# Norm rows by DMA, a late second norm and another order of issue in a hybrid RG-LRU / Mamba-2 layer

## The chip, the core and the metric

The kernel runs on one core of a Trainium2 chip. The core has a matrix engine (TensorE, PE), a vector engine (VectorE, DVE), a scalar engine (ScalarE, ACT), GpSimd (POOL) and SyncE (SP), each with its own in-order stream of instructions, and 16 DMA engines. Engines wait for each other by semaphores. On-chip data lies in SBUF, 128 partitions wide; matmul results go to PSUM. The metric is the device time of one execution in microseconds (us).

## The reference

One decoder layer on 2048 tokens of width 1024, all in fp32. A shared input projection feeds two groups of heads; their normalised outputs go through one output projection; a gated FFN of width 2816 follows. Each sub-layer has an RMS norm ahead and one behind it:

```python
h = rms_norm(x, pre_mix_norm[li]);  proj = h @ w_in[li]
lx = causal_depthwise_conv(lru_x, ...);  lh = rg_lru(lx, ...)        # gated recurrence over time
y_lru = rms_norm(lh * gelu(lru_gate), lru_out_norm[li])
xbc = silu(causal_depthwise_conv(ssd_xbc, ...))                      # x, B, C of Mamba-2
y = ssd_chunked(sx * dt[..., None], dt * A, sB, sC) + ssd_d * sx     # chunks of 128 tokens
y_ssd = rms_norm(y * silu(ssd_z), ssd_out_norm[li])
x = x + rms_norm(concatenate([y_lru, y_ssd]) @ w_out[li], post_mix_norm[li])
h = rms_norm(x, pre_ffn_norm[li])
x = x + rms_norm((silu(h @ w_gate[li]) * (h @ w_up[li])) @ w_down[li], post_ffn_norm[li])
```

`rms_norm(x, w)` is x times 1/sqrt(mean of x^2 over the width + 1e-6), times w.

## The kernel before

An fp32 product is made of three faster ones: each operand is split into a high and a low part (fp32r), and `mm3` (L136 to L139) adds hi*hi, lo*hi and hi*lo. ACT casts the high part (L132), DVE subtracts for the low one (L133). A product of the input projection is 128 output channels by 1024 tokens, 48 such matmuls of 512 columns.

The program runs in stages. Tokens come in two blocks of 1024. For each block: the Mamba-2 group (time steps dt, then B, C, then eight pairs of heads, each with a projection X and a gate Z), then the RG-LRU group. Then the output projection over 16 tiles of 128 tokens with the norm behind it, the residual and the norm ahead of the FFN; then gate and up products by Strassen's scheme (seven products instead of eight), and the down product in the same scheme. Operands of the FFN go through DRAM (`h_dr`, `f_dr`, `t_dr`).

The norm ahead of the input projection is applied after the product for the first block: the product of the unnormalised x is multiplied by `rsb`, a 128 x 1024 tile in whose every row stand the 1/rms values of the block's 1024 tokens (L295, L308). Its values come from `rms_of` (L115 to L121: eight one-column matmuls L118, then a short chain for the root) as `rtok`, a token per partition and a chunk per column. `spread` (L153 to L159) turns these into rows: DVE multiplies the identity by a column (L155), and a matmul with a matrix of ones (L158) puts the diagonal into all partitions. ACT copies the result to `rsb` (L627). For the second block `normed` (L573) uses `spread` for two half rows and multiplies x itself (L580).

Two PSUM pools serve the first half of the program: `pp` and `pq`, two buffers each. The first three products (dt, B, C) stand in pp, pp and pq; the next, X0, takes the first pp buffer that comes free, and Z0 the second, which is free once B has been multiplied by `rsb`. Weights come through four `raw` tiles (SP's queue), and split into four `s_hi` and four `s_lo` tiles.

The time-step sums (`ssd_dt3`, L436 to L460) go to DRAM as `cs_dr` (L450) and come back for every pair of heads as `L` (L511), one row to all partitions; from it the decay factors are made. In `ssd_mix` the transposes L514, state products L530, reads L542 and outputs L551 stand between the projections.

In the output stage (L785 to L822) a token tile goes through two norms: the first behind the projection (L811 Square, L813), the second ahead of the FFN (L816 Square, L818), and then through transposes into `h_dr`. For the last tile of each half of the second block the normed rows go to `hl_dr` instead (L821) and are taken up in the gate stage by `late_rows` (L855). Meanwhile `build_op` (L709) splits the first block's operands for the gate stage (casts L717, subtractions L718 into `hx` and `hy`).

At the end, `second_half` (L1043) closes each token tile: sum of the last product (L1089), its Square on ACT (L1025), multiply by the norm's gains (L1026), the root, the residual, the output.

What sets the order: the Python code says what depends on what. The framework's scheduler then lays down the stream of each engine, from its own costs of each instruction and the priorities that the code gives. `order` rows below are these streams.

## Time and profile before

| | |
|---|---|
| median of 3 runs | 2635.73 us (2632.55 to 2636.6) |
| profiled execution | 2635.64 us, its span 2633.8 us |
| PE busy | 2613.7 us (99%) |
| DVE busy | 1852.7 us (70%) |
| ACT busy | 1123.6 us (43%) |
| DMA | 357.79 MB, mean 136 GB/s |

The span is the time from the first to the last instruction in the profiled execution; the rest of its time lies around it. Busy times come from the records of single instructions. Matmuls are pipelined: a matmul of 512 columns has a record of some 0.39 us, but one starts every 0.227 us, so that start-to-start times count. Where an engine stands idle, the profile names what it waited for: in a row such as "PE pq L514 <- DVE t L546" the matmul of line 514 into a `pq` tile waited for DVE's operation of line 546 on a `t` tile.

### The profile page before, as it was taken

To read this page: it belongs to the slowest core of one execution; us is meant where nothing else is said; L and a number is where in the kernel's file an instruction comes from. 1 tells how busy PE (TensorE), PEld (TensorE's weight loads), DVE (VectorE), ACT (ScalarE), POOL (GpSimd) and SP (SyncE) were. 2 spreads that over 40 slices of the span, in tenths; PEclk is the share of its full clock that TensorE was granted. 3 is DMA by queue.
4 is the path that set the end of the run, shared out by engine and by line. 5 is a ranking of instruction groups with operands and counts; after the bars stand their busy time and mean duration, and the time that the engine had idled before them with its cause. 6 is when DMAs were issued, how large, how long until landed. Compare 5 with 4: busy or idle time off the path is not lost.

```text
span 2633.8 us, 31866 instructions
## 1 busy us (share of the span) xinstructions
PE 2613.7 (99%) x12360; PEld 2170.4 (82%) x12360; DVE 1852.7 (70%) x2716; ACT 1123.6 (43%) x1340; POOL 1.1 (0%) x8
## 2 busy tenths in 40 slices
PE   9999999999999999999999999999999999999998
PEld 7888888888888887888877888888888888888887
DVE  7997878888777767544478777678767675334676
ACT  6544456754535777332253222234222222322443
POOL 0000000000000000000000000000000000000000
PEclk9999999999999999999999999999999999999999
DMA  5342461223334635543454333235333325444664
GB/s 211 111 131 73 128 201 65 82 88 113 95 96 150 210 96 205 154 136 123 143 196 150 134 104 116 81 121 195 104 100 110 106 92 173 151 139 153 212 245 140
DMA packets 189975, 357.79 MB, mean 136 GB/s; under 512 B 18528, under 2 KB 91616, under 8 KB 189824
## 3 DMA queue, kind: packets, MB, share of 16 engines
q1 hardware_dynamic: 88912, 256.56, 30.3%
q10 hardware_dynamic: 100912, 99.20, 10.8%
q8 instruction: 97, 1.59, 0.2%
q14 instruction: 54, 0.44, 0.1%
HBM read 253.86 MB, written 101.84 MB: 135 GB/s over the span
## 4 chain that ended last, share of the span: by engine, by line
PE 93%; DVE 3%; ACT 2%; DMA 1%; issue 1%; DVEq 0%; ACTq 0%; SPq 0%
PE pf L139 16%; PE pf L138 16%; PE pf L137 16%; PE pp L137 11%; PE pp L139 10%; PE pp L138 10%; PE pq L137 3%; PE pq L138 3%; PE pq L139 3%; PE pq L530 1%; PE pq L542 1%; PE pq L551 1%; DMA t_dr<-L 1%; PE pq L514 1%; DVE t L399 0%
## 5 line engine op out<-in xcount | busy, mean ns | idle before, releaser
L137 PE MATMUL pp<-hx,s_hi 128*128 128x512 f32 x1392 | 548.2, 394 | 1.2 <-ACT hx L243 0.7
L139 PE MATMUL pp<-hx,s_lo 128*128 128x512 f32 x1392 | 545.4, 392 | 0.5 <-DVE s_lo L133 0.5
L138 PE MATMUL pp<-hx,s_hi 128*128 128x512 f32 x1392 | 543.6, 391 | 0.6 <-DVE hx L244 0.6
L132 ACT CAST s_hi<-raw 128x1024 fp32r<-128x1024 f32 (+1 forms) x167 | 170.3, 1022 | 380.2 <-PE pp L138 123.0
L139 PEld LDWEIGHTS pp<-hx,s_lo 128*128 128x128 f32 x1392 | 261.7, 188 | 56.5 <-issue 0.9
L137 PEld LDWEIGHTS pp<-hx,s_hi 128*128 128x128 f32 x1392 | 261.8, 188 | 56.2 <-issue 1.6
L138 PEld LDWEIGHTS pp<-hx,s_hi 128*128 128x128 f32 x1392 | 261.9, 188 | 54.2 <-DVE hx L244 1.0
L139 PE MATMUL pf<-hx,s_lo 128*128 128x512 f32 x704 | 273.9, 389 | 0.7 <-DVE s_lo L133 0.7
L137 PE MATMUL pf<-hx,s_hi 128*128 128x512 f32 x704 | 274.2, 389 | 0.4 <-ACT s_hi L132 0.4
L138 PE MATMUL pf<-hx,s_hi 128*128 128x512 f32 x704 | 273.9, 389 | 0.0
L133 DVE TENSOR_TENSOR s_lo<-raw,s_hi 128x1024 fp32r<-128x1024 f32 (+1 forms) x167 | 198.0, 1187 | 64.1 <-ACT s_hi L132 55.7
L978 DVE TENSOR_TENSOR d_lo<-draw,d_hi 128x1024 fp32r<-128x1024 f32 (+1 forms) x110 | 121.5, 1129 | 171.4 <-ACT d_hi L977 170.1
L132 ACT CAST s_hi<-S 128x1024 fp32r<-128x1024 f32 x86 | 90.3, 1050 | 268.6 <-PE pf L138 247.3
L138 PE MATMUL pf<-d_lo,d_hi 128*128 128x512 f32 x504 | 196.1, 389 | 0.0
L977 ACT CAST d_hi<-draw 128x1024 fp32r<-128x1024 f32 (+1 forms) x110 | 104.9, 980 | 213.5 <-PE pf L138 181.6
L139 PE MATMUL pf<-d_hi,d_lo 128*128 128x512 f32 x504 | 195.9, 389 | 0.0
L137 PE MATMUL pf<-d_hi 128*128 128x512 f32 x504 | 194.6, 389 | 0.0
L139 PEld LDWEIGHTS pf<-hx,s_lo 128*128 128x128 f32 x704 | 132.1, 188 | 28.9 <-DVE s_lo L133 1.6
L137 PEld LDWEIGHTS pf<-hx,s_hi 128*128 128x128 f32 x704 | 132.1, 188 | 28.2 <-ACT s_hi L132 0.9
L138 PEld LDWEIGHTS pf<-hx,s_hi 128*128 128x128 f32 x704 | 132.1, 188 | 27.4
L302 DVE SCALAR_TENSOR_TENSOR lx<-xr,pk,lx 128x1024 f32<-128x1024 f32 x108 | 138.2, 1279 | 10.4 <-ACT lx L299 9.3
L138 PE MATMUL pf<-hy,s_hi 128*128 128x512 f32 x356 | 138.8, 390 | 1.5 <-DVE hy L718 1.4
(339 smaller groups left out, 4518.2 us busy)
## 6 DMA issues: line engine op xcount, KB each, us to landing
raw<-w_gu_dram SPq DMA_DIRECT2D x86, 512.0 KB, 4.2
f_dr<-fo ACTq DMA_DIRECT2D x154, 256.0 KB, 4.5
raw<-w_in_dram SPq DMA_DIRECT2D x72, 512.0 KB, 3.4
draw<-f_dr SPq DMA_DIRECT2D x57, 512.0 KB, 4.3
L<-cs_dr SPq DMA_DIRECT2D x32, 512.0 KB, 5.3
g_dr<-t ACTq DMA_DIRECT2D x32, 512.0 KB, 3.4
raw<-g_dr SPq DMA_DIRECT2D x32, 512.0 KB, 5.0
raw<-h_dr SPq DMA_DIRECT2D x26, 512.0 KB, 4.4
```

What stands on the lines that cost most here:

```text
L132: a.copy(out=hi, in_=raw)
L133: v.tensor_sub(out=lo, in0=raw, in1=hi.bitcast(F32))
L137: te.matmul(o, lhsT=wh, rhs=hi, start=start, stop=False)
L138: te.matmul(o, lhsT=wh, rhs=lo, start=False, stop=False)
L139: te.matmul(o, lhsT=wl, rhs=hi, start=False, stop=stop)
L302: v.scalar_tensor_tensor(out=y, in0=xr[:, k:k + TB], scalar=cw(k), in1=y, op0=ALU.mult, op1=ALU.add)
L514: te.transpose(pt[:, c].rearrange("p j d -> p (j d)"), xc[:, c * P:(c + 1) * P], ident)
L530: te.matmul(pst[:, c, :], lhsT=Bt[:, c, :], rhs=xe[:, c].rearrange("p j d -> p (j d)"), start=True, stop=True)
L542: te.matmul(po[:, c, :], lhsT=(sc[:, xi, :] if c == 0 else U[:, c - 1, :]), rhs=C[:, c * P:(c + 1) * P], start=True, stop=True)
L551: te.matmul(py[64 * j:64 * j + 64, c, :], lhsT=xd[:, c, j, :], rhs=L[:, j, c, :], start=True, stop=True)
L977: a.copy(out=hi, in_=r)
L978: v.tensor_sub(out=lo, in0=r, in1=hi.bitcast(F32))
```

## The change

Five things change:

- `put_norm` and `get_norm` take the place of `spread`: one transpose makes the 8 x 128 row block, DVE copies it, a DMA writes it to DRAM (`r_dr`), and another reads it back to all partitions.
- The time-step sums (`ssd_dt3`) are called after the first X projection instead of ahead of `ssd_group2`, and use a `t4` tile.
- The second norm of the last token tile of each half is made in the gate stage from `x1_dr` (`late_norm`), in gate steps 3 and 5; its transposes follow in steps 4 and 6, with the gains put on by ACT.
- In the tail the last multiply writes into the PSUM tile of the product (`room`) instead of in place.
- The scheduler is told to use its detailed model of the machine (`schedule_with_timeline_sim=True`), so that the order on every engine is laid anew.

```diff
-    def spread(r, lo, n, tmp):
-        dg = tmp.rearrange("p (c t) -> p c t", t=P)[:, 0:n]
-        v.tensor_tensor(out=dg, in0=bc(ident[:, None, :], [P, n, P]), in1=bc(r[:, lo:lo + n, None], [P, n, P]), op=ALU.mult)
-        ps = pq.tile([P, TB], F32, name="pq")
-        for h in range(n // 4):
-            te.matmul(ps[:, h * HB:(h + 1) * HB], lhsT=ones, rhs=tmp[:, h * HB:(h + 1) * HB], start=True, stop=True)
-        return ps
+    def put_norm(b, row_tile):
+        ps = pq.tile([P, NC, P], F32, name="pq")
+        te.transpose(ps[0:NC, 0, :], rtok[:, b, :], ident)
+        row = row_tile()[0:NC, :]
+        v.tensor_copy(out=row, in_=ps[0:NC, 0, :])
+        sy.dma_start(out=r_dr[b], in_=row)
+
+    def get_norm(out, b, lo, n):
+        sy.dma_start(out=out, in_=r_dr[b, lo:lo + n].rearrange("c t -> (c t)").partition_broadcast(P))
...
-            ps = spread(rtok[:, b], 4 * hh, 4, t4())
+            rw = t4()[:, 0:HB]
+            get_norm(rw, b, 4 * hh, 4)
...
-        a.copy(out=rsb, in_=spread(rtok[:, 0], 0, NC, t4()))
+        put_norm(0, lambda: tp.tile([P, P], F32, name="r_row", bufs=1))
+        get_norm(rsb, 0, 0, NC)
...
-                if gi == 0:
-                    dts = ssd_dt3(b, *dtq)
-                    acc = tl.tile([P, TB], F32, name="acc", bufs=1)
                 grp = ssd_group2(*BC)
                 for i in range(4):
                     xs = ssd_proj(b, 4 * gi + i, hT)
+                    if gi + i == 0:
+                        dts = ssd_dt3(b, *dtq)
+                        acc = tl.tile([P, TB], F32, name="acc", bufs=1)
...
+                if b + 1 < NB and i == 2:
+                    put_norm(1, lambda: tp.tile([P, P], F32, name="r_row", bufs=1))
...
-            a.activation(out=junk, in_=mx, func=AF.Square, accum_out=ss[:, 1:2])
-            rstd_of(ss[:, 1:2], rs[:, 1:2], 1)
-            v.scalar_tensor_tensor(out=xnt, in0=mx, scalar=rs[:, 1:2], in1=gpf, op0=ALU.mult, op1=ALU.mult)
             b, i, j = t // NC, t % 4, (t % NC) // 4
-            if b + 1 == NB and i == 3:
-                a.dma_start(out=hl_dr[j], in_=xnt)
-            else:
+            if b + 1 < NB or i < 3:
+                a.activation(out=junk, in_=mx, func=AF.Square, accum_out=ss[:, 1:2])
+                rstd_of(ss[:, 1:2], rs[:, 1:2], 1)
+                v.scalar_tensor_tensor(out=xnt, in0=mx, scalar=rs[:, 1:2], in1=gpf, op0=ALU.mult, op1=ALU.mult)
                 turn.append(lambda b=b, i=i, j=j, xnt=xnt: turned(b, i, j, xnt))
...
+        def late_norm(j, res):
+            r = [res() for _ in range(2)]
+            t0 = (NB - 1) * TB + j * HB + 3 * P
+            ss = small.tile([P, 2], F32, name="o_ss")
+            rs = small.tile([P, 2], F32, name="o_rs")
+            for q in range(2):
+                sy.dma_start(out=r[q], in_=x1_dr[t0:t0 + P, q * HB:(q + 1) * HB])
+                a.activation(out=res(), in_=r[q], func=AF.Square, accum_out=ss[:, q:q + 1])
+            v.tensor_add(out=ss[:, 0:1], in0=ss[:, 0:1], in1=ss[:, 1:2])
+            rstd_of(ss[:, 0:1], rs[:, 0:1], 1)
+            for q in range(2):
+                v.tensor_scalar(out=r[q], in0=r[q], scalar1=rs[:, 0:1], scalar2=None, op0=ALU.mult)
+            return r
...
-                a.copy(out=xs[-1], in_=ps)
+                for k in range(4):
+                    c = slice(k * P, (k + 1) * P)
+                    a.activation(out=xs[-1][:, c], in_=ps[:, c], func=AF.Copy, scale=par("g_ffn", 4 * q + k))
...
-                if b + 1 < NB and 3 <= fi < 5:
-                    late_rows(fi - 3, res)
+                if b + 1 < NB and fi in (3, 5):
+                    late = late_norm((fi - 3) // 2, res)
+                if b + 1 < NB and fi in (4, 6):
+                    late_rows((fi - 4) // 2, late, res)
...
-            v.tensor_mul(out=y[:, t], in0=y[:, t], in1=pfw[:, e * HB:(e + 1) * HB])
+            v.tensor_mul(out=y[:, t] if room is None else room, in0=y[:, t], in1=pfw[:, e * HB:(e + 1) * HB])
...
-            second_half((m1, u2), t, 0, 0, ms[t], xq[t])
+            second_half((m1, u2), t, 0, 0, ms[t], xq[t], p)
...
-    with tile.TileContext(nc) as tc:
+    with tile.TileContext(nc, schedule_with_timeline_sim=True) as tc:
```

Rows of an order below are instructions of one engine in the order of issue: line, operation, output<-inputs with buffer numbers, shape, and xN for N alike. Lines of the changed kernel are its own (L155 there is the transpose in `put_norm`, L424 stands for L422, L516 for L514, L544 for L542, L553 for L551, L724 for L718).

First place: PE in the first projection X0 (`pp_613`, now `pp_590`) and at the head of Z0 (`pp_690`, now `pp_667`). Before:

```order
L138 MATMUL pp_613<-hx_243,s_hi_616 128x512
L158 MATMUL pq_460<-t4_458,ones_118 128x512 x2
L139 MATMUL pp_613<-hx_242,s_lo_617 128x512
...
L138 MATMUL pp_613<-hx_354,s_hi_616 128x512
L139 MATMUL pp_613<-hx_353,s_lo_617 128x512
L137 MATMUL pp_690<-hx_214,s_hi_622 128x512
L138 MATMUL pp_690<-hx_215,s_hi_622 128x512
```
Now:

```order
L138 MATMUL pp_590<-hx_346,s_hi_593 128x512
L139 MATMUL pp_590<-hx_345,s_lo_594 128x512
L155 MATMUL pq_458<-ident_113,rtok_144 8x128
L137 MATMUL pp_590<-hx_349,s_hi_593 128x512
...
L138 MATMUL pp_590<-hx_354,s_hi_593 128x512
L139 MATMUL pp_590<-hx_353,s_lo_594 128x512
L424 MATMUL pq_515<-ident_113,Bt_503 128x128 x8
L137 MATMUL pp_667<-hx_214,s_hi_599 128x512
L138 MATMUL pp_667<-hx_215,s_hi_599 128x512
```
The spreading matmuls stood behind 23 matmuls of X0. The transpose that takes their place stands behind 42, six ahead of X0's end, and the eight transposes L424 directly ahead of Z0.

Second place: PE at the end of the first block's Mamba group, where a head pair's transposes (into `pq_2385`) meet the next product. Before:

```order
L139 MATMUL pp_2256<-hx_353,s_lo_2053 128x512
L542 MATMUL pq_2311<-Cc_1574,sc_149 128x128
L542 MATMUL pq_2311<-Cc_1574,t4_2228 128x128 x7
L551 MATMUL pq_2323<-L_2141,t4_2153 64x128 x16
L514 MATMUL pq_2385<-ident_113,lx_2248 128x128 x8
L137 MATMUL pp_2405<-hx_214,s_hi_2167 128x512
L138 MATMUL pp_2405<-hx_215,s_hi_2167 128x512
```
Now:

```order
L138 MATMUL pp_2496<-hx_354,s_hi_2259 128x512
L139 MATMUL pp_2496<-hx_353,s_lo_2260 128x512
L137 MATMUL pp_2626<-hx_214,s_hi_2408 128x512
L138 MATMUL pp_2626<-hx_215,s_hi_2408 128x512
...
L138 MATMUL pp_2626<-hx_223,s_hi_2408 128x512
L139 MATMUL pp_2626<-hx_222,s_lo_2409 128x512
L516 MATMUL pq_2385<-ident_113,lx_2248 128x128 x8
L137 MATMUL pp_2626<-hx_226,s_hi_2408 128x512
```
The transposes stood at the head of the product `pp_2405`, right behind the outputs L551. Now nine matmuls of the next product (`pp_2626`) stand ahead of them.

Third place: DVE at the entry to the gate stage, where it splits the operands `hy` (L718, now L724) beside the last token tile's norm (`mx`, `xn`). Before:

```order
L90 TENSOR_SCALAR rs_v_10269<-o_ss_10248 128x1
L934 TENSOR_TENSOR ft_10315<-pf_10438,ft_10315 128x512
L718 TENSOR_TENSOR hy_10419<-raw_10416,hy_10418 128x512
L92 RECIPROCAL rs_y_10267<-rs_s_10266 128x1
L93 TENSOR_TENSOR rs_t_10268<-rs_y_10267 128x1
L94 TENSOR_TENSOR rs_t_10268<-rs_t_10268,rs_v_10269 128x1
L95 TENSOR_SCALAR rs_t_10268<-rs_t_10268 128x1
L718 TENSOR_TENSOR hy_10423<-raw_10416,hy_10422 128x512
L96 TENSOR_TENSOR o_rs_10249<-rs_y_10267,rs_t_10268 128x1
L818 SCALAR_TENSOR_TENSOR xn_10242<-mx_10244,o_rs_10249,gpf_7614 128x1024
L718 TENSOR_TENSOR hy_10429<-raw_10426,hy_10428 128x512
```
Now:

```order
L724 TENSOR_TENSOR hy_10396<-raw_10389,hy_10395 128x512
L940 TENSOR_TENSOR ft_10286<-pf_10293,ft_10285 128x512
L779 TENSOR_TENSOR S_10147<-xT_9832,S_10147 128x512
L724 TENSOR_TENSOR hy_10402<-raw_10399,hy_10401 128x512
L724 TENSOR_TENSOR hy_10406<-raw_10399,hy_10405 128x512
L94 TENSOR_TENSOR rs_t_10240<-rs_t_10240,rs_v_10241 128x1
L944 TENSOR_TENSOR ft_10287<-pf_10308,ft_10285 128x512
L133 TENSOR_TENSOR s_lo_10448<-raw_10443,s_hi_10447 128x1024
L95 TENSOR_SCALAR rs_t_10240<-rs_t_10240 128x1
L947 TENSOR_TENSOR ft_10288<-pf_10342,ft_10287 128x512
L96 TENSOR_TENSOR o_rs_10236<-rs_y_10239,rs_t_10240 128x1
L819 SCALAR_TENSOR_TENSOR mx_10231<-mx_10231,o_rs_10236,pmw_7613 128x1024
```
The rows of the second norm (a second chain for the root and L818) are gone for this tile, and the last splits stand ahead of the first norm's multiply L819 instead of behind it.

## Rows read from the trace of the kernel before

**Rows 1.** The page's first part: busy us (share of the span) xinstructions of each engine.

```profile
PE 2613.7 (99%) x12360; PEld 2170.4 (82%) x12360; DVE 1852.7 (70%) x2716; ACT 1123.6 (43%) x1340; POOL 1.1 (0%) x8
```

**Rows 2.** Windows: length; busy us of PE, PEld, DVE, ACT, POOL; clock, DMA share, GB/s.

```profile
76.00:340.00 264.00, 261.02 (x1533) 221.79 (x1533) 228.50 (x316) 117.44 (x109) 0.00 (x0) 1.00 0.39 120
...
1384.00:2220.00 836.00, 834.86 (x3688) 690.50 (x3689) 609.25 (x855) 256.75 (x339) 0.00 (x0) 1.00 0.36 120
```

**Rows 3.** PE's waits: us in total, times, longest.

```profile
PE pq L514 <- DVE t L546: 1.8, 1, 1.8
PE pf L138 <- DVE hy L718: 1.4, 2, 1.2
PE pq L443 <- DVE halo L300: 1.1, 1, 1.1
...
PE pq L118 <- DVE acc L322: 1.0, 1, 1.0
PE pp L182 <- DVE hx L172: 0.8, 1, 0.8
PE pq L138 <- DVE t L378: 0.8, 1, 0.8
...
PE pp L137 <- ACT hx L243: 0.7, 1, 0.7
PE pp L138 <- DVE hx L244: 0.6, 1, 0.6
```

**Rows 4.** Timeline of the tail, DVE: start, us, line, op [idle before <-releaser].

```profile
2625.81 0.69 DVE L1089 TENSOR_TENSOR m<-pf,m 128x512 f32<-128x512 f32 x1 [2.47 <-PE pf L139]
...
2627.35 0.69 DVE L1026 TENSOR_TENSOR m<-m,pfw 128x512 f32<-128x512 f32 x1 [0.85 <-ACT fjunk L1025]
```

**Rows 5.** Timeline of PE, 38.5 to 52.

```profile
39.15 1.84 PE L118 MATMUL pq<-ones,acc 128*128 128x1 f32 x16
...
46.19 1.88 PE L158 MATMUL pq<-t,ones 128*128 128x512 f32 x4
...
49.27 1.07 PE L422 MATMUL pq<-ident,Bt 128*128 128x128 f32 x8
```

**Rows 6.** Timeline of ACT and DVE, 47.9 to 49.5.

```profile
48.11 1.02 ACT L627 COPY rsb<-pq 128x1024 f32<-128x1024 f32 x1 [4.77 <-PE pq L158]
...
49.16 1.22 DVE L295 TENSOR_TENSOR xr<-pp,rsb 128x1024 f32<-128x1024 f32 x1 [2.10 <-ACT rsb L627]
```

**Rows 7.** Timeline of SP's queue at the time-step sums' trip to DRAM.

```profile
83.42 0.34 SPq L450 DMA_DIRECT2D cs_dr<-Bt  x1
85.33 1.76 SPq L511 DMA_DIRECT2D L<-cs_dr  x4
```

**Rows 8.** The page's last part: DMA issues, KB each, median us to landing.

```profile
raw<-w_in_dram SPq DMA_DIRECT2D x72, 512.0 KB, 3.4
...
L<-cs_dr SPq DMA_DIRECT2D x32, 512.0 KB, 5.3
```

**Rows 9.** Windows around 550 (columns as in Rows 2).

```profile
545.00:550.80 5.80, 4.83 (x30) 3.97 (x29) 5.29 (x10) 2.24 (x3) 0.00 (x0) 1.00 0.00 0
550.80:554.20 3.40, 3.40 (x10) 2.62 (x9) 3.16 (x17) 2.51 (x4) 0.00 (x0) 0.50 0.42 154
```

**Rows 10.** Timeline of DVE, entry to the gate stage.

```profile
1379.88 0.68 DVE L718 TENSOR_TENSOR hy<-raw,hy 128x512 fp32r<-128x512 f32 x1
...
1381.91 1.28 DVE L818 SCALAR_TENSOR_TENSOR xn<-mx,o_rs,gpf 128x1024 f32<-128x1024 f32 x1
```

**Rows 11.** Timeline of ACT, the last token tile's second Square.

```profile
1377.01 1.06 ACT L816 ACTIVATE ob<-mx 128x1024 f32<-128x1024 f32 x1 [1.90 <-DVE mx L814]
```

**Rows 12.** Timeline of ACT at the start.

```profile
6.75 1.04 ACT L620 ACTIVATE lx<-t 128x1024 f32<-128x1024 f32 x1
```

**Rows 13.** Timeline of PE at 78 to 80.

```profile
78.08 0.39 PE L138 MATMUL pp<-hx,s_hi 128*128 128x512 f32 x1
79.61 0.46 PE L443 MATMUL pq<-dtx,tri 128*128 128x128 f32 x2 [1.14 <-DVE halo L300]
```

More of the change, by code (lines that the diff above doesn't have):

```diff
@@ L63, in hybrid_layer @@
     h_dr = [[dram.tile([P, 4, HB], F32, name=f"h_dr{b}_{o}") for o in range(7)] for b in range(NB)]
-    hl_dr = dram.tile([2, P, D], F32, name="hl_dr")
+    r_dr = dram.tile([NB, NC, P], F32, name="r_dr")
     f_dr = [[dram.tile([P, KF, HB], F32, name=f"f_dr{b}_{o}") for o in range(7)] for b in range(NB)]
@@ L447, in ssd_dt3 @@
                 te.matmul(pr[0:NH, c * P:(c + 1) * P], lhsT=dta[:, c, :], rhs=tri, start=True, stop=True)
-            cr = tp.tile([P, NC, P], F32, name="Bt", bufs=1).rearrange("p c l -> p (c l)")[0:NH, :]
+            cr = t4()[0:NH, :]
             v.tensor_copy(out=cr, in_=pr[0:NH, :])
@@ L576, in normed @@
                 load_xT(xt, b, hh, k2)
-            ps = spread(rtok[:, b], 4 * hh, 4, t4())
+            rw = t4()[:, 0:HB]
+            get_norm(rw, b, 4 * hh, 4)
             for k in range(KD):
                 z = xt[k // 2][:, k % 2]
-                v.scalar_tensor_tensor(out=z, in0=z, scalar=par("g_pre", k), in1=ps[:, 0:HB], op0=ALU.mult, op1=ALU.mult)
+                v.scalar_tensor_tensor(out=z, in0=z, scalar=par("g_pre", k), in1=rw, op0=ALU.mult, op1=ALU.mult)
             return xt
@@ L853, in hybrid_layer, with late_rows @@
         half0 = []
-        def late_rows(j, res):
-            r = raw_tile()
-            sy.dma_start(out=r, in_=hl_dr[j])
+        def late_norm(j, res):
[11 more added lines that the diff above has]
+            return r
+        def late_rows(j, r, res):
             xs = []
@@ L861, in late_rows @@
                 for k in range(4):
-                    te.transpose(ps[:, k * P:(k + 1) * P], r[:, q * HB + k * P:q * HB + (k + 1) * P], ident)
+                    te.transpose(ps[:, k * P:(k + 1) * P], r[q][:, k * P:(k + 1) * P], ident)
                 xs.append(res())
-                a.copy(out=xs[-1], in_=ps)
+                for k in range(4):
+                    c = slice(k * P, (k + 1) * P)
+                    a.activation(out=xs[-1][:, c], in_=ps[:, c], func=AF.Copy, scale=par("g_ffn", 4 * q + k))
             put = [(B11, xs[0]), (B21, xs[1])] if j == 0 else [(B22, xs[1])]
@@ L1020, in prod_tiles, with square_mul @@
                 yield ps
-        def square_mul(y, t, e):
+        def square_mul(y, t, e, room=None):
             junk = fy.tile([P, HB], F32, name="fjunk", bufs=1)
@@ L1041, in load_x1, with second_half @@
             return xt
-        def second_half(ys, t, j, e, m, xt):
+        def second_half(ys, t, j, e, m, xt, room=None):
             rs = fy.tile([P, 1], F32, name="f_rs", bufs=2)
-            rstd_of(square_mul(ys[e], t, e), rs, 1, m)
+            rstd_of(square_mul(ys[e], t, e, room), rs, 1, m)
             for z, q in ((0, a), (1, sy)):
                 h = slice(z * HB, (z + 1) * HB)
-                v.scalar_tensor_tensor(out=xt[:, h], in0=ys[z][:, t], scalar=rs, in1=xt[:, h],
+                y = room if z == e and room is not None else ys[z][:, t]
+                v.scalar_tensor_tensor(out=xt[:, h], in0=y, scalar=rs, in1=xt[:, h],
                                        op0=ALU.mult, op1=ALU.add)
```

## The prediction

> **What bounds the kernel now.** I read the page's first line, then the table of windows, then PE's waits, and only then single stretches. The page gives PE 2613.7 us of a span of 2633.8 [rows 1], so all the time in which TensorE does nothing is 20.1 us. The windows say where it lies: in the 264 us from 76 to 340 PE lacks 3.0 us, in the 836 us of the gate stage only 1.1 [rows 2]. PE's waits name the pieces, none longer than 1.8 us [rows 3]; what the list does not hold lies at the start and behind the last matmul, whose closing chain of row sums runs from 2625.81 to the span's end [rows 4]. So this is a kernel bound by the order on one engine. A change can win only (a) matmul time that it takes out, (b) the listed waits, together about 11 us, (c) a piece of the two ends; and it loses as soon as PE waits for something that it did not wait for before. DVE is the engine nearest behind: 228.5 of 264 us in the first Mamba stretch, 87% [rows 2]. The sums below are made against the profiled execution, 2635.64 us, which is 1.84 over its span; the median of the runs shown, 2635.73, is 0.1 above it.
>
> **Norm row of the first token block: a loss.** Before, the row of 1/rms values is spread over the partitions by matmuls with a matrix of ones (L158). The L118 block runs from 39.15 to 41.0, and 23 matmuls later L158 runs, at 46.19 [rows 5]; a matmul takes 0.227 us, as 834.86 us for 3688 of them in the gate stage show [rows 2]. ACT copies the result into rsb at 48.11 and the first multiply with rsb starts at 49.16 [rows 6], while PE is still in the product X0; PE waits nowhere there. Now the row goes out to DRAM and comes back by a broadcast. In PE's new order the one small transpose stands behind 42 matmuls of X0, not 23: 41.0, plus 0.5 for the later start (below), plus 42 x 0.227 = 9.5, gives 51.0. Transpose and copy: 0.5 together, by the 0.13 us that one of the eight L422 transposes takes (1.07 / 8) and a short DVE operation. Write, then read: in the same pattern with cs_dr the read is issued 85.33 - 83.42 = 1.9 us behind the write [rows 7], so it is issued at 53.4. Landing of 512 KB: L<-cs_dr, one DRAM row read by all partitions, has a median of 5.3 us; the shortest median of any 512 KB load that I take as a bound is raw<-w_in_dram with 3.4 [rows 8]. So rsb lies ready between 56.8 and 58.7, and the multiply of 1.22 us [rows 6] ends at 58.1 to 60.0 with the handing over. PE meanwhile does 6 matmuls of X0 (1.4), eight transposes (1.1) and is at Z0 at 53.7. Z0 goes into a pp buffer that this multiply sets free, there are two, and the order puts nothing else ahead. **The new wait is 4.4 to 6.3 us; I take 5.5**, since several of the L<-cs_dr reads stand in line for each other and this one is alone, but is of that form. The two DMAs stand on SP's queue behind four weight loads whose buffers, counted through the casts, are free near 45 us; if one of them were not, the wait grows by the delay. Behind the waiting multiply on DVE stand the convolutions of B and C, about 12 us of work beside 10.9 us of Z0; the first user behind Z0 comes just in time by this, so 0 to 1 us more is possible, and it is in the reserve below.
>
> **Clock.** In the trace the granted clock fell to 0.50, the 1.2 GHz level, from 550.8 to 554.2, after a wait of 1.0 us and sixteen one-column matmuls, with PE busy 4.83 of the 5.8 us before [rows 9]; half of 3.4 us is lost in such a stretch at most, by the records 10 matmuls in it where 15 fit, 1.1 us. I take 1.4. The wait of 1.8 us near 264 had no such sequel (clock 1.00 over 76 to 340 [rows 2]). A wait of 5.5 us is longer than either, so I give a fall behind it 0.6: +0.8. In return the L118 block near 547 stands ten matmuls later in the new order; the wait goes, and the fall with it at 0.7: -1.0. Together -0.2. The Trainium skill's page "TensorE: Matmul & The Clock Gate", section "What's actually happening", says it more strictly: the slow level is the default, and only activity lifts it, so that an idle engine falls back. By that rule the price behind the new wait would be the full 1.4 us and not 0.8, and the change 0.6 us poorer; the row at 550 agrees with it, the wait at 264 shows that a short one is not enough.
>
> **Matmul time removed.** L158 has 8 records in all, four of them in 1.88 us, 0.47 each: 3.8 us on PE [rows 5]. Two transposes of 0.13 us replace them: **-3.5**. The multiplies with the identity that fed them fall away on DVE; it is not the bound there, so nothing. The row for the second block is put out a whole stage before it is read: its DMAs are hidden.
>
> **Waits that the new order removes.** [Rows 3] L514 1.8: the eight transposes now stand nine matmuls into the next product instead of at its head, and 9 x 0.227 = 2.0 covers it. L443 1.1: the time-step sums go behind the first projection of the head pair, with four matmuls of the next product ahead, but these run only after the new wait on PE, in which DVE catches up with them: gone. L118 1.0: ten matmuls later, gone. L138<-t 0.8: gone by the same kind of shift. L182 0.8: half. hx 0.7 and 0.6 near 1005: the new order puts the hi products of several rows first; I count 1.0 of 1.3. hy 1.4 at the entry to the gate stage: there DVE works off a second norm (L818, 1.28) between the casts L718 that PE waits for, and ACT its Square of 1.06 [rows 10, 11]; the change leaves both out for the two last token tiles, and the casts come first in the new order: -1.4. Sum: 1.8 + 1.1 + 1.0 + 0.8 + 0.4 + 1.0 + 1.4 = **-7.5**.
>
> **The late norm.** For two tiles it moves into the fourth to seventh gate step: 4 loads of 256 KB, 4 Squares, 2 rstd chains, 4 multiplies and 16 small scaled copies, perhaps 6 us of ACT and 4 of DVE. ACT is busy 257 and DVE 609 of 836 us there [rows 2], nothing of it feeds PE before the next token block: 0, or up to +1 if a transpose in late_rows comes before its rows.
>
> **The two ends.** Tail: the multiply with pfw started at 2627.35, although its operand was there at 2626.50; it waited for ACT's Square because both touch the same tile [rows 4]. Now it writes to PSUM and runs beside it; the sum that goes on needs the Square only: -0.5. Start: ACT's first job is now a Square of 1.04 us [rows 12] ahead of the first casts; the warm-up matmuls cover half: +0.5. If the cover holds less, +1.0; if the loads come first anyway, 0.
>
> **The reserve.** Nearly every row of PE's order has another place. In the Mamba stretches the state products L542 stand singly between the projections, each waiting for a DVE step of the chain, where before they stood in blocks. I counted one pair of heads through (28.3 us of PE: 96 matmuls of 0.227 and 6.5 us of small ones; DVE 87% busy) and found every step in time, some with only 0.2 us to spare. I set +2.5 for what such counting misses.
>
> **Sum**: 5.5 - 0.2 - 3.5 - 7.5 - 0.5 + 0.5 + 2.5 = -3.2 with the waits as the list has them. The list is short of the full cost: PE's starts lie some 0.2 to 0.4 us further apart around each wait (at 79.6 it lists 1.1 us, and the matmul before started 1.53 earlier [rows 13]), about -1.9 over the eight places. Together -5.1: **2630.5 us**.
>
> **Rivals.** (1) Slower: the chain of states on DVE becomes the bound. DVE at 87% works in order; if one multiply stands a step too late, every head pair's single L542 stops PE. There are 16 such pairs; at 0.65 us each it eats 10.4 us, and the change ends at +5.3. That is the point from which it decides; at 1 us each it is +11, 2647 us. For it speaks DVE's share, against it that PE lost only 3.0 us in the whole first stretch. Chance 0.18. (2) The row's trip is hidden: if the multiply into rsb is not what PE needs first, or the transpose comes earlier than counted, the wait of 5.5 and its clock go: 2624. The order as laid speaks against it. Chance 0.15. (3) The waits only change their places: PE is 99% busy, and what is gained at one buffer is waited for at the next; then 3.5 of matmul time stand against the wait for rsb and the reserve: 5.5 + 0.8 + 2.5 - 3.5 - 0.5 + 0.5 = +5.3 at most, more likely with a third of the waits won, +2.7: 2638. Chance 0.20. The page on the clock has no rival of its own beyond the 0.6 us.
>
> **How the numbers follow.** A measurement of this kernel cannot tell less than about 0.2%, 5.3 us, from no change. My forecast, chance 0.47, has the range 2625 to 2635 and lies on that bound: 0.25 of it counts as faster, 0.22 as the same. Rival 2 adds 0.15 to faster; rival 3 0.17 to the same and 0.03 to slower; rival 1 0.16 to slower and 0.02 to the same. Faster 0.40, same 0.41, slower 0.19. The range 2622 to 2641 leaves out the better half of rival 2 and the worse part of rival 1.
>
> **What would show it.** PE's waits should have a new first row of 4 to 7 us, a matmul into pp released by DVE's multiply with rsb, near 54 to 60 us, and perhaps a stretch at 0.50 behind it. The rows for L514, L443, hx and hy should be gone, PE's sum be lower by 3 to 4 us, and the closing multiply start beside the Square. Many short waits of L542 for DVE between 76 and 340 and between 550 and 830 would show rival 1; no wait at 54 us, rival 2.

## The result: slower by 0.6%, and the profile after

The changed kernel takes 2651.26 us (median of 4, 2646.3 to 2654.03) against 2635.76 for the kernel before in the same session: ratio 1.0059, with the interval 1.0042 to 1.0076. The forecast was 2630.5, a gain, with a range up to 2641, so it failed. The profiled execution took 2650.45 us, its span is 2648.5, 14.7 longer than before. The page's first part, of the kernel after, answers to [rows 1]:

```profile
PE 2618.5 (99%) x12354; PEld 2176.3 (82%) x12354; DVE 1848.2 (70%) x2719; ACT 1128.7 (43%) x1352; POOL 1.1 (0%) x8
```

PE is busy 4.8 us longer and idle 9.9 longer (2648.5 - 2618.5 = 30.0, before 20.1). Both halves need a cause. PE's waits of the kernel after (us in total, times, longest), against [rows 3]:

```profile
PE pp L137 <- DVE xr L297: 7.0, 2, 4.4
PE pq L137 <- ACT wob L245: 3.5, 1, 3.5
PE pq L137 <- ACT t L379: 3.2, 2, 3.0
PE pq L544 <- DVE t L537: 2.7, 1, 2.7
PE pp L137 <- DVE t L310: 2.3, 4, 1.5
```

Not one of the eight rows of [rows 3] is left. In their place stand six waits of 1.5 to 4.4 us at five places, named below by the time at which each begins. Windows of the kernel after: length; busy us of PE, PEld, DVE, ACT, POOL; clock, DMA share, GB/s. They answer to [rows 2, 9]:

```profile
57.00:61.00 4.00, 3.48 (x9) 2.79 (x10) 4.00 (x8) 3.58 (x3) 0.00 (x0) 0.57 0.11 42
76.00:340.00 264.00, 260.00 (x1453) 219.12 (x1452) 207.41 (x283) 102.93 (x95) 0.00 (x0) 0.99 0.32 101
...
141.80:149.00 7.20, 6.09 (x15) 4.77 (x16) 6.54 (x21) 1.84 (x3) 0.00 (x0) 0.56 0.21 73
...
406.50:413.00 6.50, 6.50 (x17) 5.12 (x18) 6.50 (x8) 5.72 (x6) 0.00 (x0) 0.56 0.83 272
...
1053.60:1058.00 4.40, 4.00 (x10) 2.71 (x11) 3.05 (x5) 3.96 (x6) 0.00 (x0) 0.61 1.00 298
1384.00:2220.00 836.00, 835.50 (x3693) 691.33 (x3692) 615.31 (x888) 274.25 (x369) 0.00 (x0) 1.00 0.35 119
```

The granted clock falls to its lower level, 1.2 GHz, four times, each time behind one of the waits or inside it; I call such a stretch slow. (The windows take in its edges, so their means lie above 0.50.) Length times (1 - clock), summed over the four: 4.0 x 0.43 + 7.2 x 0.44 + 6.5 x 0.44 + 4.4 x 0.39 = 9.5 us; before it was 3.4 x 0.5 = 1.7 [rows 9]. The gate stage in the last row loses 0.5 us in 836.

With that the account closes. Idle: the waits of the row's trip 4.4, at 139 us 3.4, at 343 2.6, at 400 4.5, at 1050 3.5 make 18.4; the old ones that went [rows 3] are 8.2, the tail gained 0.6 (below): +9.6 against 9.9 measured. Busy: -3.3 of matmul work (3.8 of L158 out, two L155 of 0.27 in) + 9.5 - 1.7 = +4.5 against 4.8. (In these windows PE also stands idle for some 2 us, on which 0.9 of the 9.5 fall, so the second sum is good to about 1 us.)

**The trip of the norm row, near 53 us.** The timeline of SP's queue, then DVE's, of the kernel after:

```profile
51.19 0.35 SPq L158 DMA_DIRECT2D r_dr<-r_row  x1
52.43 0.35 SPq L161 DMA_DIRECT2D rsb<-r_dr  x1
```

```profile
56.15 1.22 DVE L297 TENSOR_TENSOR xr<-pp,rsb 128x1024 f32<-128x1024 f32 x1 [0.84 <-DMA rsb<-r_dr]
```

Write to read takes 1.2 us, read to use 3.7: PE's wait of 4.4 is what the prediction's chain gave as its lower end.

**139 us.** PE and DVE of the kernel after:

```profile
142.18 0.49 PE L544 MATMUL pq<-Cc,t 128*128 128x128 f32 x2 [2.70 <-DVE t L537]
143.40 0.77 PE L137 MATMUL pp<-hx,s_hi 128*128 128x512 f32 x1 [0.74 <-DVE xr L294]
```

```profile
130.13 2.29 DVE L526 TENSOR_TENSOR L<-L,cs 128x2048 f32<-128x2048 f32 x1 [3.47 <-DMA L<-cs_dr]
...
139.45 2.28 DVE L540 TENSOR_TENSOR L<-L,SM 128x2048 f32<-128x2048 f32 x1
141.66 0.47 DVE L537 SCALAR_TENSOR_TENSOR t<-sc,aet,pq 128x64 f32<-128x64 f32 x2
```

The step that PE waits for, L537, needs 0.47 us and stands behind L540's 2.28; DVE is late because, some nine microseconds earlier, it stood 3.47 us in front of L526 for a load, and it had no idle time from there to L537 in which to make that up.

**343 us.** ACT and DVE:

```profile
332.55 1.34 ACTq L364 DMA_DIRECT2D L<-wx_dram  x2
338.65 1.91 ACT L367 CAST bd<-L 128x2048 fp32r<-128x2048 f32 x1 [8.84 <-DMA L<-wx_dram]
```

```profile
340.60 1.23 DVE L372 TENSOR_TENSOR SM<-L,bd 128x1024 fp32r<-128x1024 f32 x1 [3.90 <-ACT bd L367]
...
344.07 1.21 DVE L297 TENSOR_TENSOR xr<-pp,rsb 128x1024 f32<-128x1024 f32 x1
```

ACT stands 8.84 us in front of a cast whose block-diagonal weights are still under way, with the convolution's own step on ACT behind it; DVE then waits for the cast, and L297, which sets PE's buffer free, stands behind both.

**400 us.** PE, then the DVE work ahead of L310:

```profile
404.03 0.73 PE L137 MATMUL pq<-t,bd 128*128 128x512 f32 x2 [3.01 <-ACT t L379]
406.28 0.79 PE L137 MATMUL pp<-hx,s_hi 128*128 128x512 f32 x1 [1.52 <-DVE t L310]
```

```profile
397.43 0.68 DVE L568 TENSOR_TENSOR L<-L 128x512 f32<-128x512 f32 x1
...
398.63 2.34 DVE L401 TENSOR_TENSOR_SCAN t<-t,hc,t 128x1024 f32<-128x1024 f32 x1
400.90 1.26 DVE L304 SCALAR_TENSOR_TENSOR lx<-xr,pk,lx 128x1024 f32<-128x1024 f32 x1
```

The last step of the convolution (L304), whose cast L379 PE needs, stands behind the recurrence's scan and behind two sums for the FFN weights that nobody needs before the down product. ACT's order bears on it as well. ACT and the window of the kernel after:

```profile
398.57 1.12 ACT L388 ACTIVATE t<-pq,hb 128x1024 f32<-128x1024 f32 x1 [1.08 <-DVE L L568]
...
402.95 1.03 ACT L379 CAST t<-lx 128x1024 fp32r<-128x1024 f32 x1
```

```profile
385.00:405.00 20.00, 16.57 (x70) 12.62 (x69) 18.85 (x21) 18.69 (x18) 0.00 (x0) 1.00 0.48 171
```

ACT waited 1.08 us with the store of a sum at the head of its stream, then did four steps of the recurrence without a gap; the cast starts 0.8 us after L304's end (402.16). Both engines are nearly full here, DVE 18.85 us of 20 and ACT 18.69, while ACT was busy only 10.28 of the 20 us from 366 on: the new order bunches their work at this place.

**1050 us.** ACT:

```profile
1049.27 1.05 ACT L132 CAST s_hi<-raw 128x1024 fp32r<-128x1024 f32 x1 [5.08 <-DMA raw<-g_dr]
1052.05 1.04 ACT L132 CAST s_hi<-raw 128x1024 fp32r<-128x1024 f32 x1 [1.73 <-DMA raw<-g_dr]
1053.00 0.72 ACT L245 ACTIVATE wob<-raw,pk 128x512 fp32r<-128x512 f32 x1
```

The cast of the output weights that PE's next matmul needs stands behind two casts of a later token tile whose data is still in flight.

At 139, 343 and 1050 us an engine that works in order stands in front of something that is not there yet, with the step that PE needs behind it. At 400 it stands behind other work of the same engines.

**The tail**, DVE of the kernel after, against [rows 4]:

```profile
2640.81 0.69 DVE L1110 TENSOR_TENSOR m<-pf,m 128x512 f32<-128x512 f32 x1 [3.06 <-PE pf L139]
2641.53 0.70 DVE L1046 TENSOR_TENSOR pf<-m,pfw 128x512 f32<-128x512 f32 x1
```

L1046 follows at once instead of waiting for the Square: from the last matmul to the root's first step 1.97 us, before 2.57.

### The profile page after: what moved, and what is told of

Read it like the earlier page. It is cut to its first block, busy times and chain, and to the rows that moved or that the text cites. A ratio compares the mean times of both kernels' runs of the same rounds, so it can differ in the third digit from the quotient of the medians.

```text
span 2648.5 us, 31906 instructions
## 1 busy us (share of the span) xinstructions
PE 2618.5 (99%) x12354; PEld 2176.3 (82%) x12354; DVE 1848.2 (70%) x2719; ACT 1128.7 (43%) x1352; POOL 1.1 (0%) x8
## 3 DMA queue, kind: packets, MB, share of 16 engines
q10 hardware_dynamic: 100624, 98.15, 10.6%
## 4 chain that ended last, share of the span: by engine, by line
PE 93%; DVE 3%; ACT 2%; DMA 2%; issue 1%; ACTq 0%; DVEq 0%; SPq 0%
PE pf L137 16%; PE pf L139 16%; PE pf L138 16%; PE pp L137 11%; PE pp L138 11%; PE pp L139 11%; PE pq L138 3%; PE pq L139 3%; PE pq L137 3%; PE pq L544 1%; PE pq L553 1%; PE pq L532 1%; DVE lx L304 1%; DMA L<-cs_dr 1%; PE pq L767 0%
## 5 line engine op out<-in xcount | busy, mean ns | idle before, releaser
L304 DVE SCALAR_TENSOR_TENSOR lx<-xr,pk,lx 128x1024 f32<-128x1024 f32 x108 | 138.0, 1278 | 7.2 <-ACT lx L301 6.6
```

Source lines behind the costliest of these rows:

```text
L304: v.scalar_tensor_tensor(out=y, in0=xr[:, k:k + TB], scalar=cw(k), in1=y, op0=ALU.mult, op1=ALU.add)
```

## The experiments

Theory O: the order of issue that the detailed machine model lays down costs the time, at the places named, and the other parts gain. Rival R: the norm row's trip and its slow clock cost it. Rival D: DVE's chain of states is the bound everywhere. D could be read off at once: the list above has one wait of L544 for all sixteen pairs of heads, and DVE is busy 207 of 264 us, before 228.5 [rows 2]. All ratios are against the kernel before, run on the same chip in the same session, with 95% intervals; its median was between 2633.96 and 2634.51, so that kernels of different sessions are compared by their distance from it. The change's own is +15.5 us.

**The order alone, without the parts** (kernel before).

```
-    with tile.TileContext(nc) as tc:
+    with tile.TileContext(nc, schedule_with_timeline_sim=True) as tc:
```

> The kernel before with the scheduler's detailed model and nothing else of the change. Theory (order): the loss comes from the order of issue; it puts instructions of in-order engines behind loads that land later, PE waits some 3 us at three to five places and the clock falls behind them: 2643 to 2655 us, granted clock 0.996 or lower. Rival (parts): the rewritten parts, the row by DMA and the moved time-step sums, bring the waits: 2631 to 2638 us here, clock 0.999.

2663.77 us, 1.0111 [1.0096, 1.0127], +29.6 us: a loss as theory O has it, and larger than I expected. Its waits on PE (lines as before):

```profile
PE pp L137 <- DVE xr L295: 6.9, 3, 4.0
PE pf L137 <- ACT s_hi L132: 4.8, 1, 4.8
...
PE pq L137 <- ACT t L377: 3.2, 2, 3.0
PE pq L137 <- ACT wob L243: 3.1, 1, 3.1
```

The waits of 343, 400 and 1050 us are there without any of the parts, and one of 4.8 at 1412, in the entry to the gate stage, where this kernel has the second norms that the change moves away. Three others stand in the Mamba group: 2.5 near 54 (for the row, which is spread by matmuls here), 3.4 near 109 and 2.3 near 145.

**The parts alone, in the old order** (kernel after).

```
-    with tile.TileContext(nc, schedule_with_timeline_sim=True) as tc:
+    with tile.TileContext(nc) as tc:
```

> All rewritten parts of the change, with the scheduler's old model. Theory (order): the waits near 139, 343, 401 and 1050 us of the changed kernel are gone, only the wait for rsb may stay: 2627 to 2637 us. Rival (parts): 2645 to 2655 us.

2628.90 us, 0.9981 [0.9972, 0.9991]. The waits of this kernel on PE:

```profile
PE pp L137 <- DVE xr L297: 2.8, 1, 2.8
...
PE pq L118 <- DVE acc L324: 1.0, 1, 1.0
```

So the parts gain 5.3 us, and with them in place the order costs 20.8 (15.5 + 5.3); without them it costs 29.6. The row's wait is here 2.8, since L155 stands at 45.26 and not at 50.58; the clock behind it stays at 1.00. R falls as the main cause: this kernel has the row's trip and gains, and the one before has no such trip and loses.

**Row spread by matmuls again for the first block, the rest as after; and the same in the old order.**

```
-        put_norm(0, lambda: tp.tile([P, P], F32, name="r_row", bufs=1))
-        get_norm(rsb, 0, 0, NC)
+        a.copy(out=rsb, in_=spread(rtok[:, 0], 0, NC, t4()))
```

> The changed kernel, but with the first block's row spread by matmuls as before; new order. Both theories: the wait for rsb at 53 us (4.4 us) and the slow clock behind it (1.7 us lost) go, 1.7 us of matmul time come back. If the rest of the order stays alike: 4 us less than the changed kernel, 2645 to 2649 us. If the order shifts elsewhere, waits at other places, and the time can come out anywhere between 2636 and 2656.

> As the run before it, with the scheduler's old model: all rewritten parts but the first block's row. Theory (order): the best of the four, 2625 to 2632 us. Rival (parts, the row by DMA being the one at fault): also 2625 to 2632, and then the code-only run is 10 us or more above it; by the order theory it is 0 to 6 us above it.

New order: 2656.48, 1.0079 [1.0062, 1.0096], +22.3. That was a miss: without the row's trip the kernel is slower, not faster. The scheduler laid everything else anew; a new wait of 5.1 came near 109, the one at 343 grew from 2.6 to 4.5, and that of L552 (after: L544) from 2.7 to 3.6. Under this model an edit moves waits all over the first half, so a part's price cannot be read from one such pair. Old order: 2627.51, 0.9974 [0.9964, 0.9984], 1.4 better than with the trip, by medians whose intervals overlap.

**Mending single places, in the new order.** Each edit ties one instruction behind another, and the rest of the order stays nearly as it was. First the place at 1050: the loads of the third token tile and their casts come behind the weights' casts (`last["wo"]` holds the last of these; the lines that store it are left out, here and in the next two places).

```
...
+                with tc.issue_after(last["wo"]) if n == 0 else ExitStack():
+                    gq.append(load_g(tiles[n + 2]))
```

> The changed kernel, with one edge in the order of ACT: the casts of the third token tile's operand (its load lands late) stand behind the last casts of the output weights instead of ahead of them. Theory (late load in an in-order stream): PE's wait of 3.5 us near 1050 goes, and with it the slow stretch behind it (3.4 us at half clock, 1.7 us): 5 us less than the changed kernel, 2645 to 2648 us. Rival (the wait is ACT's load there, not its order; or the slack is used up right behind): the wait turns up a few us later, 2650 to 2653 us.

2649.72, 1.0065 [1.0049, 1.008], +15.8: no gain by time. The wait went only from 3.5 to 2.8. ACT of this kernel shows what was next in line:

```profile
1053.64 1.95 ACT L247 ACTIVATE wob<-raw,pk 128x512 fp32r<-128x512 f32 x3 [2.55 <-DMA acc_dr<-acc]
```

The casts now come first, but wait for a store (`acc_dr`, issued at 1045.88) to leave, so the late load was one of two things in the way. The slow stretch behind the place is gone; the clock is 1.00 over 1050 to 1058. By the trace the place gave 2.4 us, and the one at 343 took 3.2: its wait grew from 2.6 to 4.2, with a slow stretch behind it.

Then the place at 343 as well: the cast `bd` goes behind the convolution's first step.

```
...
+                with tc.issue_after(last["conv"]):
+                    a.copy(out=bd, in_=st)
```

> As the run before, and a second edge on ACT: the cast of the gate matrices, which waits for a load, stands behind the first recurrent projection's convolution instead of ahead of it. Theory (late load): the wait of 2.6 us near 343 goes too: 2.5 us less than the run before, 2642 to 2646 us. No slow stretch followed that wait, so nothing more. Rival: DVE's row of work there is the limit, and the time stays within 1 us of the run before.

2642.52, 1.0036 [1.0023, 1.005], +8.6: 7.2 us better than the one before it in the same session, whose wait there was 4.2 us with a slow stretch behind it. By the trace 6.1 of this come between 300 and 350 us. ACT of this kernel:

```profile
335.89 1.91 ACT L370 CAST bd<-L 128x2048 fp32r<-128x2048 f32 x1 [0.56 <-DMA L<-wx_dram]
```

ACT does its steps of the convolution first, and waits 0.56 us where it waited 8.84; PE's wait there is gone. This shows the cause of that place.

**The place at 400**, three attempts on top of the last. The FFN weights' sums behind the convolution's last step; then their stores on POOL's queue in addition; then, from the kernel before these two, the sums one per step in four steps instead of two in two (f7 in a text further on):

```
...
+                    with tc.issue_after(last["convd"]):
+                        wdn_sums(wk)
```

> As the run before, and on DVE the sums of the down weights stand behind the convolution of the same step instead of among its steps. Near 401 no load is late; DVE's order alone is to blame by the trace (two sums and a scan ahead of the convolution's last step, 3.5 us). If the sums are the deciding part the wait of 3.0 us shrinks to about 1.8 and the slow stretch behind it may go: 1 to 7 us less, 2636 to 2644 us. If the scan decides, no change: 2642 to 2646 us.

```
-                a.dma_start(out=t_dr[o][:, k, :], in_=z)
+                g.dma_start(out=t_dr[o][:, k, :], in_=z)
```

> As the run with two ACT edges and the sums moved on DVE, but the stores of the sums are issued by GpSimd instead of ACT. In that run the block had moved from DVE to ACT: a store of the sums stood on ACT's stream 2.3 us for its sum, with the cast that PE waits for behind it. Theory (the store's issue in ACT's stream): the wait of 3.5 us near 400 shrinks below 1, the slow stretch behind it goes: 5 to 7 us less than that run, 2637 to 2640 us. Rival (the scan on DVE decides): 2642 to 2645 us.

```
-WS = ((0, 2, 2, 0, 0, 0, 0, 0), (0, 2, 2, 1, 1, 1, 0, 0))
+WS = ((0, 1, 1, 1, 1, 0, 0, 0), (0, 2, 2, 1, 1, 1, 0, 0))
```

> As the run with two ACT edges, and the four sums of the down weights that stand in two steps of the first block's recurrent group, two each, stand in four steps, one each. Theory (DVE's amount of work there: 18.85 of 20 us busy): the waits of 3.0 and 1.5 us near 395 to 400 and the slow stretch go, 5 to 7 us less than that run: 2636 to 2638 us. Rival (the order alone, the scan and the casts in front of the one that PE needs): the wait stays within 1 us of what it was, 2641 to 2645 us.

2644.02 (1.0039 [1.0025, 1.0053]), 2646.01 (1.0049 [1.0035, 1.0062]) and 2643.12 (1.0031 [1.0021, 1.004]): +10.1, +12.0 and +8.6, no gain over +8.6 in any. In the first, ACT stood 2.34 us with a store behind the late sums. In the second the wait for the cast fell to 1.2, and the next one, for L312, rose to 2.8. In the third, DVE there, and PE:

```profile
390.67 2.34 DVE L404 TENSOR_TENSOR_SCAN t<-t,hc,t 128x1024 f32<-128x1024 f32 x1
...
394.18 1.21 DVE L406 TENSOR_TENSOR t<-t,t 128x1024 f32<-128x1024 f32 x1
395.31 1.22 DVE L402 SCALAR_TENSOR_TENSOR t<-t,lx 128x1024 f32<-128x1024 f32 x1
...
396.51 1.21 DVE L312 TENSOR_TENSOR t<-pp,rsb 128x1024 f32<-128x1024 f32 x1
```

```profile
397.78 0.79 PE L137 MATMUL pp<-hx,s_hi 128*128 128x512 f32 x1 [3.51 <-DVE t L312]
```

No sum stands there any more, and PE waits 3.5 us all the same (once, where it was 3.0 and 1.5), now for L312 behind the scan and its multiplies. So the sums alone are not the cause. In the 20 us up to 398 DVE is busy 18.85 us here and ACT 19.84: with both engines full, taking one step away brings up the next. That the place of the recurrence's steps is what costs is argued, not shown; an order without them at this spot was not tried.

**The row's trip put first**: its three steps at high priority, which places L155 at 40.51 us.

```
+        with tc.high_priority(offset=HQ):
+            rms_of(acc, rtok[:, 0])
+            put_norm(0, lambda: tp.tile([P, P], F32, name="r_row", bufs=1))
+            get_norm(rsb, 0, 0, NC)
```

> The changed kernel, with the first block's norm sums, transpose and both DMAs at high priority; the transpose stands ahead of X0 instead of behind 42 of its matmuls. Theory (the row's trip is too long only because it starts late): the wait of 4.4 us at Z0 and the slow stretch behind it go, 6 us less than the changed kernel, 2644 to 2647 us. Rival (PE stands at the transpose instead, for the short chain of the root): a wait of 2 to 3 us at 41 us, 2647 to 2650 us.

2646.14, 1.0048 [1.0034, 1.0061], +12.1 where the change had +15.5. By the trace the kernel is 6.1 us ahead of the changed one at 67 us and 5.2 at 116. The wait and the slow stretch behind it are both gone, the multiply starts at 46.95. By medians the gain is 3.4. So the trip costs 4.4 of waiting and its clock, unless it is issued early; then PE does not wait for it.

**Is the slow clock the wait's doing?** Fifteen small matmuls (two records each in the trace) whose results nobody reads fill the hole at 53 us.

```
+                for n in range(15):
+                    te.matmul(pt[:, n % 8, 64:128], lhsT=ones, rhs=ones[:, 0:64], start=True, stop=True)
```

> The changed kernel, with 15 matmuls of 64 columns without use (a few us of PE) put into the wait for rsb ahead of Z0; their results are not read. Theory (the clock falls because PE stands idle): Z0 starts no later, the slow stretch at 57 to 61 us is gone, 1.7 us less than the changed kernel, 2648 to 2651 us. Rival (the clock falls for another reason, or such small matmuls do not count): the granted clock there stays at 0.5, 2650 to 2653 us.

2649.27, 1.0064 [1.0049, 1.008], +15.3: by time no difference that these runs can show. The trace shows one. PE and the window of this kernel:

```profile
53.74 3.56 PE L433 MATMUL pq<-ones 128*128 128x64 f32 x30 [0.58 <-DVE dt L431]
57.55 0.47 PE L137 MATMUL pp<-hx,s_hi 128*128 128x512 f32 x1 [0.25 <-DVE xr L297]
```

```profile
57.00:61.00 4.00, 3.75 (x18) 3.05 (x18) 4.00 (x8) 3.54 (x3) 0.00 (x0) 1.00 0.11 40
```

The data come at the same time, 18 matmul records stand where 9 were, the clock stays at 1.00, and at 67 us the kernel is 1.4 us ahead of the one it was made from. The idle time makes the fall, and the fall costs 1.4 on top of the wait.

**All mends together** (both edges on ACT, the sums one per step, and the row put first).

> As f7, with the norm sums, the transpose and both DMAs of the first block's row at high priority as well: all the repairs together. Theory (the loss is the sum of its places): 5 to 6 us less than f7, so 2630 to 2632 us if f7 comes out by its theory, 2636 to 2640 otherwise; what is left are the places near 140 and 1050 us. Rival (the order has no slack, a repair at one place is lost at the next): within 2 us of f7.

2639.17, 1.0012 [1.0003, 1.0022], +4.7: of the loss of 15.5 us, 10.8 are taken back. Putting the row first gives 4.0 here, in one session with the kernel without it. Its list of waits still begins with

```profile
PE pp L137 <- DVE t L312: 3.7, 2, 3.5
PE pq L547 <- DVE t L540: 3.2, 1, 3.2
PE pq L137 <- ACT wob L247: 3.1, 1, 3.1
```

and a slow stretch follows each of the three.

**Where the parts gain.** The late norm and the closing multiply, alone on the kernel before (in part; both stand whole in the diff of the change):

```
...
-            if b + 1 == NB and i == 3:
-                a.dma_start(out=hl_dr[j], in_=xnt)
...
+                if b + 1 < NB and fi in (3, 5):
+                    late = late_norm((fi - 3) // 2, res)
...
+            v.tensor_mul(out=y[:, t] if room is None else room, in0=y[:, t], in1=pfw[:, e * HB:(e + 1) * HB])
```

> The kernel before, old model of the scheduler, with the two rewritten parts at its end alone: the late second norm and the closing multiply into PSUM. The waits of 3.4 us at the entry to the gate stage go, and 0.5 to 0.7 us at the tail: 2630 to 2632 us by my sum. If they bring nothing, 2633 to 2636 us, and the gain of 6.7 us of all parts together lies in the Mamba stages.

2628.93, 0.9982 [0.9973, 0.9991], -5.1: more than I expected, and nearly all that the parts together gain. The window at the entry to the gate stage, of this kernel and then of the kernel before (columns as in [rows 2]):

```profile
1370.00:1400.00 30.00, 30.00 (x134) 24.84 (x133) 29.38 (x42) 14.52 (x20) 0.00 (x0) 1.00 0.53 181
```

```profile
1370.00:1400.00 30.00, 27.32 (x114) 20.73 (x113) 27.77 (x49) 17.94 (x27) 0.00 (x0) 1.00 0.54 189
```

134 records stand against 114; PE's idle time of 2.7 us is gone. Against the same matmuls of the kernel before, this one is 0.4 us ahead at the output stage's end, 3.2 at 1386 us, 5.7 at 1430 and 4.8 from 1485 on, when the late norm begins to run.

**A version that beats both.** The parts in the old order, the first block's row by matmuls, and the sums of squares of block 0 one `yield`, by the trace twelve matmuls of 512 columns and sixteen of 128, later, which aims at the wait for L118 near 547 [rows 3, 9]:

```
                     yield
+                    yield
                     sumsq(b, 0, acc)
```

> All rewritten parts but the first block's row, old model of the scheduler, and the sixteen one-column matmuls of the first block's norm sums (L118 near 545) some fifteen matmuls later. They waited 1.0 us, and a stretch of 3.4 us at half clock followed. Theory: wait and slow stretch go together, 1.0 + 1.6 = 2.6 us less than the same kernel without the edit, 2624 to 2626 us. Rival: the one-column matmuls by themselves let the clock fall, wait or not: only 1.0 us less, 2626 to 2627 us, and the slow stretch moves along with them.

2623.95, 0.9965 [0.9952, 0.9977]. The wait of 1.0 and the slow stretch are gone together:

```profile
540.00:552.00 12.00, 12.00 (x71) 10.42 (x70) 11.66 (x27) 7.46 (x7) 0.00 (x0) 1.00 0.22 71
```

By the trace the place gave 2.6 us, more than the 1.0 that the list of waits shows. The sixteen records of L118 stand at 547.81 here, with the clock at 1.00, so they do not lower it by themselves.

## Why the prediction was wrong, step by step

- **What bounds the kernel: held.** The time is the order of PE's work and its holes; the account above closes with holes and clock alone.
- **The row's trip: held.** Forecast 4.4 to 6.3, taken as 5.5, measured 4.4: the read was issued 1.2 behind the write, not 1.9 [rows 7], and its 3.7 to the use are near the shortest bound of 3.4 [rows 8]. It is no longer on the path when it is issued ten microseconds earlier.
- **Clock: too cheap.** I priced one possible fall at 0.6 x 1.4. The price was right where it was tested (1.4), but there were four falls, two of them twice as long, and the term of -0.2 became +7.8. Behind the row's wait the stricter rule held, that of the Trainium skill's page "TensorE: Matmul & The Clock Gate", section "What's actually happening": an idle engine falls back and activity lifts it. The filled hole agrees: the clock stays at 1.00 over 57 to 61 us, where it was 0.57. So told, the rule does not sort the short waits: behind 2.6 at 343 in the kernel after the clock did not fall, nor behind 2.8 at 53 in the parts alone, but it did behind 2.0 near 268 in the run with the late norm alone. (The wait of 1.8 without a fall, which the prediction puts near 264, ends at 269.25 in the trace.)
- **Matmul time removed: held**, -3.3 against -3.5.
- **Waits that the new order removes: the removal held, and this half of the sum was not enough.** All eight rows of [rows 3] went, 8.2 us. But I took an order in which the old waits vanish for an order without waits. It has four new places, 14.0 us of idle time, and slow clock behind three of them, 9.5 - 1.7 = 7.8 with the one behind the row. The further -1.9 for starts that lie apart around each old wait was not separated by any run; the account closes to about 1 us without it.
- **The reserve: the step that failed.** +2.5 was set for the waits that counting misses, after counting one steady pair of heads. In its place the trace has 14.0 us of new waits, and most of the 7.8 us of slow clock follow them. The steady pair does hold: of sixteen pairs only one makes PE wait for more than half a microsecond, 3.4 us near 139. The other 10.6 us stand at the changes of work: the entry to the RG-LRU group (343), its first recurrence beside a projection (400), the start of the output stage (1050). Nothing there was counted, and the durations alone would not have given it: at 343 and 1050 ACT waits for loads whose landing an order does not show. The late load is shown as the cause at 343, and as one part of it at 1050; at 400 the cause stays open.
- **The late norm: sign held, size too small.** Priced at -1.4 and 0 to +1; measured -5.3 at the entry (from 0.4 us ahead to 5.7), against +0.9 in the stage that it moves to. hy and L818 [rows 3, 10] were not the whole of what the norms held up; PE's 2.7 us of idle time in 30 were there to be read.
- **The ends: held.** The tail gained 0.6 (forecast 0.5). At the start the first matmul came 0.7 later, by 46 us 0.1 (forecast 0.5).
- **The rivals.** (1) had the size, +11 at its upper price, but not the place: no wait per pair. (2) is what putting the row first makes of that term, but not this order. (3), waits that change places, was the mechanism, held there to +2.7: it let old waits return at their old size, and new ones were larger.

What stays open: PE's wait at 139 us measured 0.5 to 3.5 in kernels with nearly the same order around it. In eight of them (the changed kernel, the mends and the row put first) DVE waits there for `L<-cs_dr`, from 1.31 to 4.31 us, and PE's wait is each time 0.6 to 0.8 shorter, from 0.54 to 3.48; in the ninth, with the useless matmuls, ACT waits 7.55 for `t<-cs_dr` and PE 3.09. So the landing of these reads sets it, by this row of traces and not by a test. It fits the wide spread of the changed kernel's runs (2646.3 to 2654.03) but does not prove it; a third `L` buffer was not tried.

## What to carry to other kernels

When a scheduler's cost model is exchanged, count the places where one kind of work gives way to another, not the steady loop: there an in-order engine can stand in front of a load that is still in flight, and what the slowest engine needs stands behind it. Measure the parts of such a change under the old order first, since here they gained 0.2% that the new order hid under a loss of 0.8%. And price a wait on TensorE with the slow clock that may follow it; here 18.4 us of waiting brought 9.5 us of it.

## What the runs showed of the hardware

- The lower clock did not follow the length of a wait alone. It followed waits of 4.4 us (53), 3.0 and 1.5 close together (400), 3.5 (1050) and 2.7 and 0.7 close together (139), and in the kernel before one of 1.0 with sixteen records of one-column matmuls behind it [rows 9]; it did not follow 2.6 (343), 2.8 (53, parts alone) and 2.8 (1050, first mend). Nor does the length sort the waits of the other runs: behind 2.0 (near 268, late norm alone), 2.5 (near 54, order alone) and 2.6 (near 1059, row by matmuls in the new order) it fell, behind 2.9 (near 1046, second mend) it did not.
- Useless small matmuls in a hole of 4.4 us kept the clock at 1.00 and were worth 1.4 us by the trace.
- A row written to DRAM and read back by all partitions (512 KB) took 1.2 us from write to the read's issue and 3.7 to its use on an idle queue; with the queue of the parts alone the read was issued 3.9 us behind the write.
